# Splitting the projected queries and keys into two parts on GpSimd in SBUF instead of on ScalarE and VectorE out of PSUM

## The chip, the cores and the metric

The kernel runs on one core of one Trainium2 chip. The metric is the device time of one execution, in microseconds. The engines are named as the profile names them: PE (TensorE, matmuls), PEld (its weight loads), DVE (VectorE), ACT (ScalarE), POOL (GpSimd) and SP (SyncE, which here issues loads).

## What is computed

One layer of a decoder trunk on 2048 tokens of width 1024: sparse attention, then a SwiGLU feed-forward part, each followed by a layer norm of `alpha * x + sublayer(x)`. What matters here is the first half of the layer:

```
proj = h @ w_in                          # q (16 heads x 64) | c_kv (256) | q_idx (8 x 64) | k_idx (64) | w_idx (8)
c_kv = rms_norm(c_kv, g)
rel   = relu(einsum(q_idx * 64**-0.5, k_idx))     # per index head
score = sum over index heads of w_idx * rel       # causal
sel   = the 256 best keys of each query           # top-k
...
attention over the selected keys, logits from q, w_uk and c_kv, values from c_kv and w_uv
```

## The kernel before, in words

Matmuls that must be accurate in float32 are made of three: each operand is split into a high part `hi`, rounded to the type that PE multiplies (`F32R`), and a low part `lo`, the rest (value minus `hi`), and `mm3` (L208 to L214) adds up hi x hi, hi x lo and lo x hi in one PSUM bank, over the contraction in pieces of 128.

The tokens are done in four quarters of 512. For each quarter `index_part` (L273) transposes x, projects the index key and four tiles of index queries, and makes the compressed keys; `scores` (L323) makes the index scores of each block of 128 queries; `kv_part` (L359) makes eight tiles of keys and eight of values; `heads_part` (L349) projects the eight tiles of attention queries. Their order is given by the list ORDER: `i0 w0 k0 h0 i1 k1 i2 k2 i3 k3 h3 h2 h1` (i: index part and scores, w: weights of keys and values, k: keys and values, h: heads, with the number of the quarter).

A projected tile of 128x512 goes as follows. `load_split` (L158 on) brings 512 KB of weights by SP's queue and splits them on POOL: a scaled copy to `whi` (L166), then a subtraction to `wlo` (L137, in the helper `split_lo`). `mm3` makes 24 matmuls into one of two PSUM banks of the tag `mm`. Then `evac` (L258) takes the tile out: ACT copies it, scaled, to `evh` (L261), DVE computes the scaled value minus `evh` into `evl` (L262), reading PSUM again, and ACT's queue issues a store of each part to memory (L263, L264; `store` is `nc.scalar`). There are 80 such tiles: 16 of index queries (memory tensor `qis`), 32 of keys (`ks`), 32 of queries (`qs`). `evh` and `evl` have three buffers each (NEV = 3). The tag `evh` also serves the index key (L284) and the tag `evl` the value tiles (L377), which ACT copies to plain f32 (L378).

What stands beside it: the scores load the index queries back from `qis` by SP's queue (`qd`, L332), multiply (L338, two double banks `big`), ACT takes the result out through Relu (`rl`, L340), DVE adds it up into S (L343 for the first head, L345 for the others), and POOL masks the diagonal when a block is complete (L347). Top-k is a bisection on S: for some blocks of queries on DVE (count `jv` L412, step `g` L414 and `t` L415), for others on ACT (`ja` L423, `ga` L425, `ta` L426, started by a POOL memset, L405), with the preparation of the second search on POOL and DVE (L438, L440) and the selection at the end (L452 to L462). It is entered with a late priority. Attention (L465 on) follows from about 720 us; its copies of S to `sm` on POOL (L508) and the feed-forward part, where POOL makes `wl` (L137) and combinations of results that ACT's queue stores (L837), come later.

Waits, buffers and the order of the instructions on each engine come from a planner. It takes the program's order as priority (`later()` puts work behind everything else that is ready) and plays the program through with modelled times, giving each engine, as it comes free, the first instruction by priority that is ready; every engine, and every queue that issues DMAs, then works strictly in the order so found. All engines wait on the chip for the real end of what they depend on.

Of the kernel before, what the change touches and what calls it, by code (L numbers as in the profile page):

```python
# [11 lines left out]
F32 = mybir.dt.float32  # L12
F32R = mybir.dt.float32r
# [6 lines left out]
AF = mybir.ActivationFunctionType  # L20
ALU = mybir.AluOpType
# [4 lines left out]
P = 128  # L26
# [12 lines left out]
QUART = 512  # L39
# [9 lines left out]
NEV, NRL, NRAW = 3, 2, 2  # L49
# [23 lines left out]
def trunk(tc, x, w_in, w_uk, w_uv, kv_g, w_o, w_gu, w_down, lm_g, lm_b, lf_g, lf_b, out, stop=99):  # L73
    nc = tc.nc
# [55 lines left out]
    def f(ap):  # L130
        return ap.bitcast(F32)
# [4 lines left out]
    def split_lo(lo, src, hi, eng=None):  # L136
        (eng or nc.vector).tensor_tensor(out=lo, in0=src, in1=f(hi), op=ALU.subtract)  # L137
# [119 lines left out]

    def evac(pe, o, scale, dst, tok):  # L258

        hi, lo = (pe.tile([P, QUART], F32R, name=t, tag=t, bufs=NEV) for t in ("evh", "evl"))  # L260
        nc.scalar.activation(hi, o, AF.Copy, scale=scale)  # L261
        nc.vector.scalar_tensor_tensor(lo, o, scale, f(hi), op0=ALU.mult, op1=ALU.subtract)  # L262
        store.dma_start(out=dst[0, :, tok], in_=f(hi))  # L263
        store.dma_start(out=dst[1, :, tok], in_=f(lo))  # L264

# [7 lines left out]
    def index_part(pp, pq, pe, bk, st, t):  # L273
# [14 lines left out]
        for j in range(IH // 2):  # L288
            c0 = OFF_QI + j * P
            o = proj_tile(pp, bk, xx, [(lambda v: v, w3[:, :, c0:c0 + P])])  # L290
            evac(pe, o, 0.125, qis[:, j * P:(j + 1) * P], tok)
# [57 lines left out]
    def heads_part(pp, pe, bk, t, xx):  # L349

        t0 = t * QUART
        tok = slice(t0, t0 + QUART)
        if xx is None:
            xx = reloaded(pp, "x", xs[t], XB)
        for j in range(NPAIR):
            o = proj_tile(pp, bk, xx, [(lambda v: v, w3[:, :, j * P:(j + 1) * P])])
            evac(pe, o, 0.125, qs[j], tok)
# [643 lines left out]
    def pool(name, side="left"):  # L1001
        cm = tc.tile_pool(name=name, bufs=1, side=side, reuse_waits="tile")
        opened[name] = cm
        return cm.__enter__()
# [25 lines left out]
    with Banks("psb", big=(2, 2)) as big:  # L1030
        pe = pool("pe")
# [85 lines left out]
```

## Time and profile before

| | us |
|---|---|
| median of 3 runs (lowest, highest) | 3292.48 (3291.38, 3297.17) |
| the profiled execution, its own time | 3283.43 |
| its span, first to last instruction | 3281.7 |
| busy: PE | 3035.7 (93%) |
| busy: PEld | 2280.4 (69%) |
| busy: DVE | 2160.8 (66%) |
| busy: ACT | 1799.9 (55%) |
| busy: POOL | 1563.3 (48%) |

Busy time is an average over stages with different limits, so it has to be cut by stretches of the span. "Idle before" is the time for which an engine stood still ahead of an instruction, with the instruction that ended it. In a chain of waits, each piece is the work that the next one waited for. Spans of POOL are rough.

### The profile page before, as it was taken

The numbers are of one execution on the slowest core, as the hardware profiler recorded it, in microseconds if no ns is written. First come the engines' busy times: TensorE is split into PE (matmuls) and PEld (weight loads), VectorE is DVE, ScalarE is ACT, GpSimd is POOL, SyncE is SP. The second block draws the span as 40 slices with busy tenths as digits, with TensorE's granted clock in tenths as the row PEclk, the third lists the DMA queues.
The fourth block names the chain that finished last, engine by engine and source line by source line (L and its number), as shares of the span: only waits on it lengthen the run. The fifth ranks groups of instructions, "written<-read, shape, count | busy, mean of one in ns | idle before, by whom it ended". The sixth has DMA issues, their size and how long they took to land.

```text
span 3281.7 us, 45310 instructions
## 1 busy us (share of the span) xinstructions
PE 3035.7 (93%) x15067; PEld 2280.4 (69%) x15067; DVE 2160.8 (66%) x3304; ACT 1799.9 (55%) x3536; POOL 1563.3 (48%) x1309
## 2 busy tenths in 40 slices
PE   8988888878888889999999989999989999999996
PEld 6766776655555556666557767888868888888875
DVE  4749979998899545544436676555676555346289
ACT  2646886797899997766662223333333333333333
POOL 3424224543232334433325546666776666645475
PEclk9999999989899999999999999999989999999998
DMA  9776554644344543766536744322233222655353
GB/s 302 226 229 202 183 183 150 219 138 107 99 131 128 136 133 112 201 159 169 153 109 206 232 133 141 107 99 100 99 121 116 103 100 100 211 165 172 111 162 135
DMA packets 460442, 499.00 MB, mean 152 GB/s; under 512 B 51120, under 2 KB 331824, under 8 KB 460208
## 3 DMA queue, kind: packets, MB, share of 16 engines
q1 hardware_dynamic: 368992, 359.09, 38.0%
q10 hardware_dynamic: 91216, 137.01, 11.5%
q8 instruction: 120, 1.97, 0.3%
q14 instruction: 114, 0.93, 0.1%
HBM read 359.01 MB, written 136.97 MB: 151 GB/s over the span
## 4 chain that ended last, share of the span: by engine, by line
PE 62%; DVE 18%; ACT 6%; DMA 6%; issue 4%; POOL 1%; SPq 1%; ACTq 0%; DVEq 0%; POOLq 0%
PE mm L213 9%; PE mm L212 9%; PE mm L214 9%; PE oc L545 7%; PE tp L541 7%; PE big L518 6%; DVE jv L412 3%; PE mm L910 2%; PE mm L908 2%; PE mm L909 2%; ACT ja L423 2%; DVE S L345 2%; ACT sm L523 1%; PE mm L691 1%; DMA aqd<-qs 1%
## 5 line engine op out<-in xcount | busy, mean ns | idle before, releaser
L508 POOL TENSOR_SCALAR sm<-S 128x768 f32<-128x768 f32 (+7 forms) x384 | 334.9, 879 | 625.8 <-PE tp L541 556.2
L212 PE MATMUL mm<-ch,wh 128*128 128x512 f32 x1232 | 484.9, 395 | 15.0 <-ACT ch L721 14.5
L213 PE MATMUL mm<-cl,wh 128*128 128x512 f32 x1232 | 489.8, 398 | 8.8 <-DVE cl L137 7.4
L214 PE MATMUL mm<-ch,wl 128*128 128x512 f32 x1232 | 486.3, 395 | 0.0
L519 DVE CUSTOM_DVE_ANT_0 sm<-big,sm 128x1024 f32<-128x1024 f32 (+7 forms) x256 | 233.8, 921 | 226.5 <-POOL sm L508 136.7
L543 ACT COPY pt<-tp 128x512 f32<-128x512 f32 (+1 forms) x559 | 303.7, 567 | 143.9 <-PE tp L541 131.0
L523 ACT ACTIVATE sm<-sm,mx 128x768 f32<-128x768 f32 (+7 forms) x384 | 346.1, 910 | 44.9 <-DVE mx L519 44.6
L541 PEld LDWEIGHTS tp<-ident,sm 128*128 128x128 f32 x2176 | 237.0, 143 | 188.0 <-issue 178.2
L541 PE MATMUL tp<-ident,sm 128*128 128x128 f32 x2176 | 362.6, 290 | 2.7 <-ACT pt L543 1.8
L423 ACT ACTIVATE ja<-S,ta 128x896 int8<-128x896 int16 (+7 forms) x224 | 317.3, 1416 | 30.6 <-DVE evl L262 8.6
L137 POOL TENSOR_TENSOR wl<-s,wh 128x512 fp32r<-128x512 f32 x176 | 239.1, 1364 | 193.5 <-ACT wh L774 193.5
L412 DVE TENSOR_SCALAR_CACHE_REDUCE jv<-S,t 128x640 int8<-128x640 int16 (+7 forms) x224 | 302.9, 1352 | 4.3
L518 PE MATMUL big<-kka,aqd 128*128 128x512 f32 (+3 forms) x896 | 237.5, 388 | 58.9 <-DMA aqd<-qs 27.9
L774 ACT CAST wh<-s 128x512 fp32r<-128x512 f32 x176 | 109.0, 620 | 331.6 <-PE mm L214 94.3
L212 PEld LDWEIGHTS mm<-ch,wh 128*128 128x128 f32 x1232 | 233.5, 190 | 72.6 <-ACT ch L721 18.3
L213 PEld LDWEIGHTS mm<-cl,wh 128*128 128x128 f32 x1232 | 234.2, 190 | 64.6 <-DVE cl L137 11.7
L214 PEld LDWEIGHTS mm<-ch,wl 128*128 128x128 f32 x1232 | 234.2, 190 | 49.3 <-POOL wl L137 0.2
L545 PE MATMUL oc<-pt,vva 128*64 128x256 f32 (+1 forms) x1536 | 236.2, 402 | 25.1 <-ACT pt L543 19.6
L137 POOL TENSOR_TENSOR wl<-wr,wh 128x512 fp32r<-128x512 f32 x132 | 190.5, 1444 | 93.9 <-ACT wh L774 92.5
L137 POOL TENSOR_TENSOR cl<-hx,ch 128x512 fp32r<-128x512 f32 (+2 forms) x106 | 153.2, 1448 | 152.3 <-ACT ch L903 132.8
L518 PEld LDWEIGHTS big<-kka,aqd 128*128 128x128 f32 x896 | 156.9, 199 | 95.4 <-DVE mx L519 48.4
L903 ACT CAST ch<-hx 128x512 fp32r<-128x512 f32 (+2 forms) x158 | 95.0, 611 | 215.7 <-PE tp L909 95.2
(279 smaller groups left out, 6794.9 us busy)
## 6 DMA issues: line engine op xcount, KB each, us to landing
wr<-in_f_w_gu SPq DMA_DIRECT2D x44, 1024.0 KB, 5.1
gs<-cc ACTq DMA_DIRECT2D x154, 256.0 KB, 2.0
hx<-gs SPq DMA_DIRECT2D x144, 256.0 KB, 3.0
aqd<-qs SPq DMA_DIRECT2D x256, 128.0 KB, 3.2
wraw<-in_a_w_in SPq DMA_DIRECT2D x56, 512.0 KB, 4.3
kka<-ks SPq DMA_DIRECT2D x96, 256.0 KB, 4.3
hx<-in_f_w_down SPq DMA_DIRECT2D x66, 256.0 KB, 3.0
qd<-qis SPq DMA_DIRECT2D x112, 128.0 KB, 4.4
```

What stands on the lines that cost most here:

```text
L137: (eng or nc.vector).tensor_tensor(out=lo, in0=src, in1=f(hi), op=ALU.subtract)
L212: nc.tensor.matmul(o, lhsT=lh, rhs=rh, start=(i == 0), stop=False)
L213: nc.tensor.matmul(o, lhsT=lh, rhs=rl, start=False, stop=False)
L214: nc.tensor.matmul(o, lhsT=ll, rhs=rh, start=False, stop=(i == n - 1))
L412: nc.vector.tensor_scalar(out=junk[:, :L], in0=data(b), scalar1=t[b], scalar2=lim - (L - TOPK), op0=ALU.is_lt, op1=ALU.add, accum_out=col( ...
L423: nc.scalar.activation(junk[:, :L], data(b), AF.Sign, bias=t[b], scale=-1.0, accum_out=ca)
L508: nc.gpsimd.tensor_scalar(out=sm[:, :wn], in0=S[b0 + i][:, w0:w0 + wn], scalar1=slope, scalar2=1.0, op0=ALU.mult, op1=ALU.mult)
L518: nc.tensor.matmul(o[:, s0:s0 + n], lhsT=qd[:, c, i * P:(i + 1) * P], rhs=kk[wi_][e][:, s0:s0 + n], start=(c == 0), stop=(c == 1))
L523: nc.scalar.activation(sm[:, :wn], sm[:, :wn], AF.Exp, bias=mx[:, i, nw - 1:nw], scale=-1.0, accum_out=su[:, i, e, wi_:wi_ + 1])
L541: nc.tensor.transpose(tp[:, at:at + P], prob(e, i, kb), ident)
L543: pcopy(pt[:, :2 * n], tp[:, :2 * n])
L545: nc.tensor.matmul(ob[e * HD:(e + 1) * HD, i0 * P:256], lhsT=vv[kb][:, e * HD:(e + 1) * HD], rhs=pt[:, e * n:(e + 1) * n], start=(kb == 0) ...
```

## The change

`evac` alone is changed. ACT copies the PSUM tile, scaled, to a plain f32 tile `raw`, which has the buffers of the tag `evl`. POOL then copies it to `hi` (tag `evh`), rounded, and subtracts: `lo` = `raw` - `hi`, written over `raw` in place. `lo` is the same memory read as F32R. DVE no longer takes part, and PSUM is read once. The two stores, their order and their queue stay.

```diff
     def evac(pe, o, scale, dst, tok):
 
-        hi, lo = (pe.tile([P, QUART], F32R, name=t, tag=t, bufs=NEV) for t in ("evh", "evl"))
-        nc.scalar.activation(hi, o, AF.Copy, scale=scale)
-        nc.vector.scalar_tensor_tensor(lo, o, scale, f(hi), op0=ALU.mult, op1=ALU.subtract)
+        raw = pe.tile([P, QUART], F32, name="evl", tag="evl", bufs=NEV)
+        hi = pe.tile([P, QUART], F32R, name="evh", tag="evh", bufs=NEV)
+        lo = raw.bitcast(F32R)
+        nc.scalar.activation(raw, o, AF.Copy, scale=scale)
+        nc.gpsimd.tensor_scalar(out=hi, in0=raw, scalar1=1.0, scalar2=1.0, op0=ALU.mult, op1=ALU.mult)
+        split_lo(lo, raw, hi, nc.gpsimd)
         store.dma_start(out=dst[0, :, tok], in_=f(hi))
         store.dma_start(out=dst[1, :, tok], in_=f(lo))
```

`split_lo(lo, src, hi, eng)` (L136, L137) is one subtraction, `eng.tensor_tensor(out=lo, in0=src, in1=f(hi), op=ALU.subtract)`; `f` reads a tile as plain f32.

## Rows read from the trace of the kernel before

**Rows 1.** The page's second part: the span in 40 equal slices of 82 us, one digit each, the busy tenths of TensorE's matmuls and of VectorE.

```profile
PE   8988888878888889999999989999989999999996
DVE  4749979998899545544436676555676555346289
```

**Rows 2.** Busy time of each engine by stretch of the span (start:end in us, its length, then busy us and the number of instructions of each engine, granted TensorE clock, DMA share and GB/s).

```profile
0.00:280.00 280.00, 236.01 (x1078) 187.22 (x1079) 165.87 (x324) 133.31 (x303) 93.56 (x105) 0.95 0.83 255
280.00:720.00 440.00, 385.07 (x1724) 309.49 (x1722) 411.44 (x578) 353.30 (x734) 174.14 (x124) 0.95 0.55 171
1240.00:3282.00 2042.00, 1978.72 (x9628) 1510.11 (x9624) 1170.71 (x1669) 842.93 (x1514) 1111.91 (x871) 0.98 0.45 141
```

**Rows 3.** The chain of waits, its shares by line, first of 0 to 280 us and then of 280 to 720 us.

```profile
by line: DMA qd<-qis 10.7%; PE mm L212 9.6%; PE mm L213 9.3%; PE mm L214 9.0%; DMA wraw<-in_a_w_in 6.6%; issue 6.4%; DMA S<-in_x 4.4%; PE big L338 4.2%; ACT ja L423 3.6%; SPq L332 2.9%; DMA wlo<-wkv 2.7%; DMA xs<-xl 2.6%; POOL wlo L137 2.6%
...
by line: DVE jv L412 18.3%; DVE S L345 14.6%; issue 10.1%; DVE g L414 5.0%; DVE evl L262 4.7%; PE mm L212 4.2%; DVE t L415 3.9%; PE mm L213 3.8%; PE mm L214 3.7%; PE big L338 3.6%; DVE S L343 2.5%; DVE S L440 2.5%; DVE ft L459 2.2%; ACT rl 
```

**Rows 4.** The instructions of line 262 over the whole span (times are min/median/max in ns), and who waited for them (us, number of waits).

```profile
L262 DVE SCALAR_TENSOR_TENSOR evl<-mm,evh x80: 666/687/693, 28.7 to 710.7; 128x512 fp32r<-128x512 f32 x80
...
  PE mm L212: 17.9, 19
  ACT ga L425: 10.2, 6
  ACT ja L423: 8.6, 3
...
  ACT ta L426: 3.8, 3
  ACT rl L340: 1.7, 2
```

**Rows 5.** Groups of instructions by line, 0 to 720 us: the copy of the value projections, out of PSUM to plain f32 (busy us, mean ns of one, idle before).

```profile
L378 ACT COPY ve<-mm 128x512 f32<-128x512 f32 x32 | 18.8, 587 | 9.1 <-PE mm L214 2.7 <-issue 2.4 <-DVE S L433 2.3
```

**Rows 6.** VectorE's busy time on line 262 alone, 280 to 720 us (the columns of rows 2).

```profile
280.00:720.00 440.00, 32.87 (x48) 0.95 0.55 171
```

**Rows 7.** Groups of instructions on GpSimd with 128x512 tiles: the one scaled copy of that shape from 0 to 720 us, and the page's subtractions in the feed-forward part.

```profile
L508 POOL TENSOR_SCALAR sm<-S 128x512 f32<-128x512 f32 x1 | 0.6, 617 | 0.1
...
L137 POOL TENSOR_TENSOR wl<-s,wh 128x512 fp32r<-128x512 f32 x176 | 239.1, 1364 | 193.5 <-ACT wh L774 193.5
```

**Rows 8.** The timeline (start us, duration us, engine, line), first with GpSimd busy, then with GpSimd idle.

```profile
605.27 3.24 POOL L137 TENSOR_TENSOR wlo<-wraw,whi 128x1024 fp32r<-128x1024 f32 x1
606.80 1.74 DVE L414 TENSOR_SCALAR g<-cnt 128x2 f32<-128x2 f32 x1
...
690.84 0.16 DVE L414 TENSOR_SCALAR g<-cnt 128x2 f32<-128x2 f32 x1
691.04 0.16 DVE L415 SCALAR_TENSOR_TENSOR t<-g,t 128x2 f32<-128x2 f32 x1
691.11 1.28 DVE L345 SCALAR_TENSOR_TENSOR S<-rl,wi,S 128x1024 f32<-128x1024 f32 x1
```

**Rows 9.** Groups by line and shape on VectorE, 280 to 720 us.

```profile
L345 DVE SCALAR_TENSOR_TENSOR S<-rl,wi,S 128x1024 f32<-128x1024 f32 x24 | 33.8, 1411 | 0.0
L414 DVE TENSOR_SCALAR g<-cnt 128x2 f32<-128x2 f32 x55 | 31.4, 570 | 0.6
L415 DVE SCALAR_TENSOR_TENSOR t<-g,t 128x2 f32<-128x2 f32 x55 | 20.5, 373 | 1.3
```

**Rows 10.** Groups by line and shape on GpSimd, 280 to 720 us: the split of the weights.

```profile
L137 POOL TENSOR_TENSOR wlo<-wraw,whi 128x1024 fp32r<-128x1024 f32 x33 | 88.5, 2683 | 2.4
L166 POOL TENSOR_SCALAR whi<-wraw 128x1024 fp32r<-128x1024 f32 x33 | 41.2, 1248 | 118.6 <-PE mm L213 85.7 <-PE mm L214 32.8
L137 POOL TENSOR_TENSOR wlo<-wraw,whi 128x1056 fp32r<-128x1056 f32 x4 | 10.5, 2615 | 0.3
```

**Rows 11.** The instructions of line 837 over the whole span, GpSimd results that ScalarE's queue stores, and who waited for them (us, number of waits).

```profile
L837 POOL TENSOR_TENSOR cc<-cc x88: 1282/1297/1747, 1997.7 to 2831.4; 128x512 f32<-128x512 f32 x88
...
  ACT wh L774: 31.3, 21
```

**Rows 12.** The timeline of GpSimd where projection tiles follow each other closely (idle time before an instruction and what ended it in brackets).

```profile
46.90 1.08 POOL L166 TENSOR_SCALAR whi<-wraw 128x1056 fp32r<-128x1056 f32 x1 [2.24 <-PE mm L214]
48.06 2.47 POOL L137 TENSOR_TENSOR wlo<-wraw,whi 128x1056 fp32r<-128x1056 f32 x1
52.16 1.08 POOL L166 TENSOR_SCALAR whi<-wraw 128x1056 fp32r<-128x1056 f32 x1 [1.63 <-PE mm L213]
```

**Rows 13.** From the instructions that touch the tile evl: its stores' time from issue to landing.

```profile
DMA to landing us min/median/max: 2.3/4.2/7.4
```

**Rows 14.** The instructions of line 261 in the four bursts of key projections (min/median/max ns, first and last start).

```profile
L261 ACT ACTIVATE evh<-mm x8: 598/599/602, 76.7 to 91.4; 128x512 fp32r<-128x512 f32 x8
...
L261 ACT ACTIVATE evh<-mm x8: 593/598/639, 224.1 to 249.8; 128x512 fp32r<-128x512 f32 x8
...
L261 ACT ACTIVATE evh<-mm x8: 623/712/787, 349.7 to 368.1; 128x512 fp32r<-128x512 f32 x8
...
L261 ACT ACTIVATE evh<-mm x8: 581/601/636, 463.9 to 482.0; 128x512 fp32r<-128x512 f32 x8
```

**Rows 15.** Who waited for whom from 0 to 720 us (us in total, times, longest us).

```profile
POOL S L347 <- DVE S L345: 84.9, 7, 21.3
...
PE mm L212 <- POOL whi L166: 4.3, 2, 3.5
```

## The prediction

> **What bounds the kernel now.** I read the slices of the page first: up to about 1240 us PE stands at 7 to 9 tenths, mostly 8, with VectorE (DVE) at 9 for long runs; after that PE is at 9 or more nearly throughout [rows 1]. So the part before 1240 us is the one that can give time back. I cut it where the work changes [rows 2]. Up to 280 us (projections of the first half of the tokens) PE is busy 236.0 us and DVE 165.9. From 280 to 720 us (the other projections and the index scores, with top-k as filler) DVE is busy 411.4 of 440 us, 94%, GpSimd (POOL) only 174.1. After 720 us the changed lines no longer run; after 1240 us PE is busy 1978.7 of 2042 us. The chain of waits says the same [rows 3]: in the first stretch it runs through loads and matmuls, and its largest item is the reload of index queries (qd), 10.7%; in the second its largest items are DVE's, jv L412, S L345, g L414, and the instruction that the change removes, evl L262, has 4.7%.
>
> How evl hurts [rows 4]: there are 80, of 687 ns. PE waited for them 17.9 us in 19 waits, because they are the last readers of a PSUM bank and there are two banks; ScalarE (ACT) waited 10.2 + 8.6 + 3.8 + 1.7 = 24.3 us, because the store of the low part stands in ACT's queue ahead of other work.
>
> **The change, part by part.** A difference of under 0.2%, 6.6 us, counts as no change: about what a measurement of this kernel can tell.
>
> ACT's copy keeps its 128x512 form, about 600 ns now [rows 14]; a copy to plain f32 of that form took 587 ns [rows 5]. Nothing.
>
> Removed from DVE: 80 x 0.687 = 55 us, of which 48 instructions, 32.9 us, in the stretch that DVE bounds [rows 6].
>
> Added to POOL: a scaled copy of 128x512, 0.62 us, and a subtraction of 128x512, 1.36 us [rows 7]: 1.98 us a tile, 158 us in all, 95 us of it between 280 and 720 us, where POOL then has 174 + 95 = 269 of 440 us. There is room. What the work costs others is in the next items.
>
> DVE pays for a busy POOL. The two-element instruction g L414, started at 606.80 us while POOL's wlo (605.27, 3.24 us) ran, took 1.74 us and ended 0.03 us after it; with POOL idle, at 690.84 us, it took 0.16 [rows 8]. Over the second stretch that makes, for g, 55 x (570 - 160 ns) = 22.6 us, for t L415, 55 x (373 - 160) = 11.7, for the widest S, 24 x (1411 - 1280) = 3.1: 37 us lost [rows 8, 9], beside 140 us of whi and wlo on POOL [rows 10]. By busy time the new work would cost 37 x 95 / 140 = 25 us. But a DVE instruction waits only for what is left of POOL's, so the loss goes with the square of POOL's length: 48 x (0.62² + 1.36²) = 107 against 37 x (1.25² + 2.68²) = 323, a third, 12 us. I take 22, near the upper end, because the narrower S are left out of the 37. The removed evl itself was never stretched, 666 to 693 ns [rows 4]. So DVE's net is -33 + 22 = -11 us (-21 to -8). Projections and scores wait for S; jv is filler. S has 14.6% of the chain beside jv's 18.3% [rows 3], a share of 0.44, so -5 us counts (-9 to -3.5).
>
> [...] If POOL's 95 us blocked DVE for all their length, DVE's -11 would be +62 us; the rows above show 37 us for 140, not 140.
>
> PE's bank comes free at the end of ACT's copy instead of evl's. Late next is the copy itself, behind ACT's other work. Of 17.9 us I let 3 stay: -15 us (-18, or only -5 if ACT itself gets late).
>
> ACT's queue: both stores wait for POOL now, the second for 1.98 us at least, and behind them stand rl L340, for which the scores wait, the top-k steps and the next copy. The nearest row is POOL's L837, whose result ACT stores: 88 instructions for which ACT waited 31.3 us [rows 11], 0.36 each. 80 x 0.36 = 28 us in place of 24: +4. Bounds: no such wait, -24; 0.36 for each of the two steps, 57 us, +33. I take one wait a tile because the wait of the first store is part of the second's.
>
> POOL behind PE: where tiles follow each other closely, POOL spends 3.55 us a tile on weights and waits 2.24 and 1.63 us for PE in between [rows 12]. The new 1.98 us just fill that gap: +2 us over the few such tiles (0, or +8 where DVE slows POOL).
>
> Index queries go to memory and back before the scores: their low part leaves 0.62 + 1.36 - 0.69 = 1.3 us later, once for each of four quarters, and the reload is on the chain [rows 3]: +4 us (0 if other PE work covers it, +12 with POOL inside a wlo). No DMA is added, and the queue that issues them is the same; SP's queue holds nothing of the change but that reload.
>
> The raw tile takes a place in the ring of three that held evl, from ACT's copy to the landing: 0.6 + 0.62 + 1.36 + 4.2 us to land [rows 13] = 6.8, or 2.3 us a tile. In the four bursts of eight key tiles the copies start 2.1, 3.7, 2.6 and 2.6 us apart on average [rows 14], so only the first is held up: 7 x 0.2 = 1.4, say +2 us (with every landing at 7.4 us, 3.3 a tile: 7 x (1.2 + 0.7 + 0.7) = +18).
>
> Sum: -15 - 5 + 4 + 2 + 4 + 2 = -8 us. The profiled execution took 3283.43 us, for a span of 3281.7; it lies 9 us below the median of the three runs, 3292.48, and I apply the difference to the median: 3284.5 us.
>
> **Rivals.** *ACT stands behind POOL* (slower). The place is the second store: POOL works in order, and when it sits in a wlo, or in L347, which waited for DVE up to 21.3 us [rows 15], the pair comes late and all of ACT with it. Price: ACT +33, bank only -12, DVE -5, the three small items +8: +24, 3316.5 us. It decides from the point where the pair ends, on average, later after the copy than evl does now. For it: POOL stood 84.9 us in L347. Against it: PE lost only 4.3 us to whi from the same queue [rows 15].
>
> *The lock eats it* (no change). It costs 25 us, DVE nets -8, of which -3.5 counts; the bank gives -10, because ACT's copies stand behind rl, and rl behind S; the other items +12: -1.5, 3291 us. For it: 37 us are lost already. Against it: the new instructions are half as long. [...]
>
> *The bank does not come free sooner* (slower; the change then does less than it says). The ring of three is full, and the copy waits for a landing. Landings of 7.4 us cost +18 for +2: -8 + 16 = +8, 3300.5 us. For it: the first burst is already at 2.1 us. Against it: the median landing.
>
> *All of it is collected* (faster). Bank -18, DVE -9, half of ACT's 24, -12, small items +4: -35, 3257.5 us. For it: DVE at 94%. Against it: it needs every favourable bound at once.
>
> **How the numbers follow.** Forecast, a small gain: 0.42, of which 0.11 ends under 6.6 us, since it lies only 1.4 us beyond; all collected 0.10; lock 0.20; ACT behind POOL 0.22; ring 0.06. Faster 0.31 + 0.10 = 0.41; same 0.11 + 0.20 = 0.31; slower 0.28. The forecast's own range is 3272 to 3290 us. The range for 8 in 10 takes in the larger gain almost whole and the ACT rival: 3258 to 3318 us; it is also that wide because the order on every engine is planned anew from modelled times.
>
> **What would show it.** Between 280 and 720 us: no evl on DVE and DVE's busy time some 11 us lower, g and t longer on average than 570 and 373 ns; PE's waits for evl gone, with no like sum for the copy; ACT's waits for the two POOL steps near 28 us; a slightly larger share of qd in the first chain. I am wrong if ACT waits for POOL 50 us or more, if copies wait for landings of stores, if PE waits for whi or wlo more than some 10 us, or if the stretches after 720 us change their length.

## The result and the profile after

The changed kernel takes 3335.26 us (median of 4, 3333.15 to 3342.36) where the kernel before takes 3291.93 (median of 4): 1.0132 times as long, 95% interval 1.0110 to 1.0155, some 43 us slower. The forecast was 3284.5 us, a small gain; 3335 also lies above the range. The profiled executions stand at 3334.10 us (span 3332.3) and 3283.43 us, 50 us apart. In the changed kernel every line number behind `evac` is 3 higher than before (S L348, rl L343, g L417, t L418); the copy is L263, the two GpSimd steps L264 and L137 (tile evl).

The page's slices of the changed kernel, 83 us each, here with GpSimd's row, and below them busy time by stretch (columns as in [rows 2]).

```profile
PE   7887888887788899999999999999989999999996
DVE  3649979997989636444445666555585555336289
POOL 4754457674333334433333636666676666645475
```

```profile
0.00:280.00 280.00, 229.34 (x1036) 181.73 (x1037) 141.09 (x276) 126.64 (x292) 156.20 (x167) 0.93 0.81 250
280.00:720.00 440.00, 381.63 (x1689) 300.51 (x1689) 411.67 (x516) 332.70 (x692) 281.14 (x204) 0.96 0.54 167
720.00:1240.00 520.00, 420.60 (x2467) 266.40 (x2465) 407.01 (x726) 464.69 (x975) 177.16 (x212) 0.90 0.43 120
1240.00:3340.00 2100.00, 2025.02 (x9880) 1540.30 (x9878) 1195.27 (x1708) 877.48 (x1580) 1138.42 (x887) 0.98 0.45 140
```

Against [rows 2], PE has 42 matmuls fewer done by 280 us and some 76 by 720 us. VectorE, which lost 48 subtractions in the second stretch, is as busy in it as before (411.67 us for 411.44) with 62 instructions fewer: its time was not freed, it was refilled. ScalarE does 20.6 us less work there, so top-k falls behind (its last count on ScalarE ends at 1243 us instead of 1206), and the attention stage that follows is late too. Over the whole span PE is busy 3056.6 us instead of 3035.7 for the same matmuls: the granted clock fell from 0.968 to 0.959 of full speed in the mean. That is 21 of the 50 us; PE's idle time, 275.7 us instead of 246.0, is the other part.

The waits to 760 us, by engine, picked out (us in total, times, longest).

```profile
PE big L341 <- ACT rl L343: 40.1, 40, 3.9
...
PE mm L212 <- POOL whi L166: 12.1, 5, 5.8
PE mm L212 <- ACT evl L263: 11.3, 9, 2.3
...
PE mm L214 <- POOL wlo L137: 8.8, 7, 2.2
...
ACT rl L343 <- DVE S L348: 41.5, 27, 5.5
...
ACT evl L263 <- POOL evl L137: 7.7, 4, 3.5
...
DVE S L346 <- POOL wi L310: 19.5, 1, 19.5
```

Two chains are to be seen. VectorE's S is late, so ScalarE waits 41.5 us for it (24.1 before) to refill the two buffers of rl, and the scores' matmuls wait 40.1 us for rl (26.5 before). And GpSimd's other products are late: PE waits 12.1 and 8.8 us for the two parts of weights (4.3 and 2.1 before, the first in [rows 15]), and S waits 19.5 us for wi, a small scaling on GpSimd of the index heads' weights (6.5 before). That one wait costs PE little by itself: PE was busy 17.7 of the 19.5 us, with projections. Nor do such rows prove a loss: e1 below has a good part of them (ScalarE 36.9 us for S, PE 15.8 for weights, S 13.8 for wi) and is faster than the kernel before.

GpSimd's own steps, to 760 us, and what they waited for; the last line is the landing time of the tile's stores.

```profile
L264 POOL TENSOR_SCALAR evh<-evl x80: 608/625/2068, 29.2 to 745.2; 128x512 fp32r<-128x512 f32 x80
L137 POOL TENSOR_TENSOR evl<-evl,evh x80: 1261/1298/2816, 29.9 to 747.0; 128x512 fp32r<-128x512 f32 x80
...
  ACT evl L263: 76.4, 25
...
DMA to landing us min/median/max: 2.3/3.4/7.8
```

The shortest and the median steps are those of [rows 7], but the longest are 2 to 3 times as long: in the mean a copy took 0.88 us and a subtraction 1.51. And the queue of GpSimd, which works in order (a subtraction whose copy ended at 331.58 us ran only at 336.66, behind a step of top-k that had stood 3.47 us for VectorE), stands 76.4 us in front of the copies that it waits for.

VectorE to 720 us: S, the subtraction, g and t, picked out (busy us, mean ns, idle before), first before the change, then after it.

```profile
L345 DVE SCALAR_TENSOR_TENSOR S<-rl,wi,S 128x768 f32<-128x768 f32 (+5 forms) x161 | 169.7, 1064 | 21.4 <-ACT rl L340 20.4
...
L262 DVE SCALAR_TENSOR_TENSOR evl<-mm,evh 128x512 fp32r<-128x512 f32 x80 | 54.9, 687 | 48.1 <-ACT evh L261 41.4 <-DMA qd<-qis 4.8 <-DMA ks<-evl 1.6
L414 DVE TENSOR_SCALAR g<-cnt 128x2 f32<-128x2 f32 (+1 forms) x92 | 37.0, 402 | 1.5
L415 DVE SCALAR_TENSOR_TENSOR t<-g,t 128x2 f32<-128x2 f32 (+1 forms) x92 | 36.3, 395 | 2.3
```

```profile
L348 DVE SCALAR_TENSOR_TENSOR S<-rl,wi,S 128x768 f32<-128x768 f32 (+5 forms) x153 | 184.0, 1210 | 32.8 <-ACT rl L343 31.6
...
L418 DVE SCALAR_TENSOR_TENSOR t<-g,t 128x2 f32<-128x2 f32 (+1 forms) x88 | 50.6, 575 | 2.2
L417 DVE TENSOR_SCALAR g<-cnt 128x2 f32<-128x2 f32 (+1 forms) x88 | 35.2, 400 | 1.7
```

At the counts of before, the longer S and t cost 161 x 0.146 + 92 x 0.180 = 40 us: of the 54.9 us that left VectorE, 15 are truly gone. The timeline (start us, length us) shows one such case.

```profile
582.80 2.01 POOL L137 TENSOR_TENSOR evl<-evl,evh 128x512 fp32r<-128x512 f32 x1
...
583.58 1.25 DVE L418 SCALAR_TENSOR_TENSOR t<-g,t 128x2 f32<-128x2 f32 x1
```

t, two columns wide, ends 0.02 us after GpSimd's subtraction; and that subtraction, 2.01 instead of 1.26 us long, had itself been held up: the S before it had run from 582.15 to 583.66. Both sides pay.

### The profile page after: what moved, and what is told of

Its sections match the earlier page's. It is cut to its first block, busy times and chain, and to the rows that moved or that the text cites. A ratio compares the mean times of both kernels' runs of the same rounds, so it can differ in the third digit from the quotient of the medians.

```text
span 3332.3 us, 45438 instructions
## 1 busy us (share of the span) xinstructions
PE 3056.6 (92%) x15067; PEld 2288.9 (69%) x15067; DVE 2155.0 (65%) x3224; ACT 1801.5 (54%) x3536; POOL 1752.9 (53%) x1469
## 3 DMA queue, kind: packets, MB, share of 16 engines
q10 hardware_dynamic: 91216, 137.01, 11.3%
## 4 chain that ended last, share of the span: by engine, by line
PE 64%; DVE 17%; DMA 6%; issue 5%; ACT 5%; POOL 3%; SPq 0%; ACTq 0%; DVEq 0%; POOLq 0%
PE mm L212 9%; PE mm L214 9%; PE mm L213 9%; PE oc L548 8%; PE tp L544 7%; PE big L521 6%; DVE jv L415 3%; PE mm L913 3%; PE mm L911 3%; PE mm L912 3%; DVE S L348 2%; DMA aqd<-qs 2%; ACT ja L426 1%; DVE cl L137 1%; PE mm L694 1%
## 5 line engine op out<-in xcount | busy, mean ns | idle before, releaser
L212 PE MATMUL mm<-ch,wh 128*128 128x512 f32 x1232 | 492.2, 401 | 16.3 <-ACT ch L724 14.9
L137 POOL TENSOR_TENSOR wl<-s,wh 128x512 fp32r<-128x512 f32 x176 | 238.6, 1360 | 193.2 <-ACT wh L777 193.2
L137 POOL TENSOR_TENSOR wl<-wr,wh 128x512 fp32r<-128x512 f32 x132 | 190.5, 1444 | 97.8 <-ACT wh L777 92.7
L137 POOL TENSOR_TENSOR cl<-hx,ch 128x512 fp32r<-128x512 f32 (+2 forms) x106 | 154.7, 1463 | 149.5 <-ACT ch L906 128.2
L348 DVE SCALAR_TENSOR_TENSOR S<-rl,wi,S 128x768 f32<-128x768 f32 (+5 forms) x161 | 196.8, 1230 | 32.8 <-ACT rl L343 31.6
```

Of the source, the lines that this page charges most:

```text
L212: nc.tensor.matmul(o, lhsT=lh, rhs=rh, start=(i == 0), stop=False)
```

## The experiments

Five ideas stood against each other: ScalarE stands behind GpSimd at its stores; the two engines hold each other up (stretching, the lock of the expectations); GpSimd's queue brings its other products late; it is the removal that is worth little; each tile has a fixed price. "Taken out" kernels, which do not compute the low part, tell the worth of the removal apart from the price of the added work. All results, with GpSimd's busy time and the mean S (147 to 161 of them) from 0 to 720 us of each profile:

| kernel | median us | ratio to before (95%) | GpSimd us | S ns |
|---|---|---|---|---|
| before | 3291.9 | 1 | 267.7 | 1064 |
| changed | 3335.3 | 1.0132 (1.0110 to 1.0155) | 437.3 | 1210 |
| e1_no_lo | 3283.9 | 0.9975 (0.9956 to 0.9994) | 277.0 | 1162 |
| e2_no_lo_pair | 3325.3 | 1.0094 (1.0060 to 1.0129) | 442.2 | 1225 |
| e3_no_lo_pair_prev | 3328.9 | 1.0111 (1.0080 to 1.0142) | 440.5 | 1246 |
| e4_stores_sp | 3338.9 | 1.0139 (1.0108 to 1.0169) | 442.3 | 1237 |
| e5_no_lo_memsets | 3311.8 | 1.0052 (1.0034 to 1.0070) | 428.0 | 1170 |
| e6_pool_late_heads | 3313.6 | 1.0056 (1.0032 to 1.0080) | 326.2 | 1124 |
| e7_pool_all_else | 3313.9 | 1.0059 (1.0036 to 1.0082) | 385.6 | 1192 |
| e8_lo_on_dve | 3321.4 | 1.0088 (1.0061 to 1.0115) | 315.8 | 1113 |
| e9_no_lo_tiny | 3293.4 | 0.9995 (0.9978 to 1.0011) | 299.2 | 1171 |
| e10_reload | 3275.6 | 0.9956 (0.9939 to 0.9973) | 180.2 | 1039 |
| e11_reload_pool | 3259.0 | 0.9907 (0.9894 to 0.9919) | 233.4 | 1058 |
| e12_quarters | 3357.7 | 1.0202 (1.0183 to 1.0221) | 489.7 | 1175 |
| e13_reload_all | 3292.1 | 0.9996 (0.9984 to 1.0008) | 356.2 | 1168 |
| e14_reload_no_lo | 3242.9 | 0.9848 (0.9834 to 0.9861) | 180.7 | 1055 |
| e15_reload_later | 3276.8 | 0.9956 (0.9941 to 0.9971) | 321.7 | 1141 |
| e16_reload_first | 3279.3 | 0.9959 (0.9944 to 0.9974) | 223.5 | 1052 |
| e17_reload_dve_time | 3271.4 | 0.9942 (0.9922 to 0.9962) | 184.8 | 1048 |
| e18_reload_dve_lumps | 3272.4 | 0.9949 (0.9930 to 0.9967) | 189.7 | 1033 |

Differences between two experiments are differences of their ratios, times 3292 us; each ratio is to the runs of the kernel before on the same chip; such a difference carries some 6 to 15 us of uncertainty, and every kernel has its own planned order.

**e1_no_lo**: only the removal.

```diff
-        hi, lo = (pe.tile([P, QUART], F32R, name=t, tag=t, bufs=NEV) for t in ("evh", "evl"))
+        hi = pe.tile([P, QUART], F32R, name="evh", tag="evh", bufs=NEV)
         nc.scalar.activation(hi, o, AF.Copy, scale=scale)
-        nc.vector.scalar_tensor_tensor(lo, o, scale, f(hi), op0=ALU.mult, op1=ALU.subtract)
         store.dma_start(out=dst[0, :, tok], in_=f(hi))
-        store.dma_start(out=dst[1, :, tok], in_=f(lo))
+        store.dma_start(out=dst[1, :, tok], in_=f(hi))
```

> The kernel before with VectorE's step taken out and nothing put in its place: the low part is not computed, and the high part is stored twice. It prices the removal alone. My theory: the removal itself is worth something, 10 to 35 us (VectorE 55 us less, PE's 17.9 us of waits for evl gone), so 3257 to 3282 us, and the 43 us that the change lost come from what it adds on GpSimd. The rival, that the new order of the plan or the earlier release of the banks is itself harmful, wants 3300 us or more here.

The removal alone, with all that waited for the subtraction and no price paid, gives 0.0025, 8 us (2 to 14). It is not free of stretching: with no work added to GpSimd (busy 277.0 us for 267.7), the mean S grew from 1064 to 1162 ns and ScalarE's wait for S from 24.1 to 36.9 us. The added time of S lies beside the splits of weights, which are the same in both kernels: measured from the shortest instruction of each width, S lost 28 us beside whi and wlo in e1 and 13 us before. So these rows move without any added work; every kernel has its own order.

**e2_no_lo_pair** (behind e1's stores):

```diff
+        dm = pe.tile([P, QUART], F32, name="evl", tag="evl", bufs=NEV)
+        nc.gpsimd.tensor_scalar(out=dm, in0=f(hi), scalar1=1.0, scalar2=1.0, op0=ALU.mult, op1=ALU.mult)
+        split_lo(dm, f(hi), dm.bitcast(F32R), nc.gpsimd)
```

> The run without the low part, plus the pair of GpSimd instructions of the change, made from the high part into a tile that nobody reads; the stores do not wait for it. It holds everything that the change puts on GpSimd and nothing that waits for its results. If VectorE is shut out by GpSimd (lock) or GpSimd stands at the pair with the weights behind it (queue), this is as slow as the change, 3320 to 3340 us. If the stores, ACT's queue or the ring of three tiles that wait for the pair are the cause, it stays near the run without the pair, 3260 to 3290 us.

The pair's results are awaited by nobody (only its buffers are, for 2.3 us), and it still costs 0.0119, 39 us, of the 51 that separate the changed kernel from e1. What must be explained is mostly the price of GpSimd's time, not of waiting for its results. Nor are the weights late here: PE waits 10.8 us for whi and wlo, less than the 15.8 in e1, which is 39 us faster.

**e3_no_lo_pair_prev**: as e2, but the pair reads the tile before.

```diff
+        last = before.get("hi")
+        hi = before["hi"] = pe.tile([P, QUART], F32R, name="evh", tag="evh", bufs=NEV)
...
-        nc.gpsimd.tensor_scalar(out=dm, in0=f(hi), ...)
+        nc.gpsimd.tensor_scalar(out=dm, in0=f(last), ...)
```

> As the run with the unread pair, but the pair works on the high part of the tile before, which has long been in SBUF, so that GpSimd need not stand and wait for ACT's copy. Lock theory: VectorE is shut out as often, so as slow as the other pair run within 10 us. Queue theory: GpSimd's idle time at the pair (76.4 us for L264 in the changed kernel) and PE's waits for whi and wlo fall, and at least half of the difference between the pair run and the run without a pair goes.

This was meant to take away GpSimd's standing still for ScalarE's copy. It did not: the planner issues the pair as early as its order allows, and GpSimd's queue stood 98.9 us for evh. As a test of the queue it is inconclusive.

**e4_stores_sp**: the changed kernel, with both stores issued by SP's queue.

```diff
-        store.dma_start(out=dst[0, :, tok], in_=f(hi))
-        store.dma_start(out=dst[1, :, tok], in_=f(lo))
+        nc.sync.dma_start(out=dst[0, :, tok], in_=f(hi))
+        nc.sync.dma_start(out=dst[1, :, tok], in_=f(lo))
```

> The changed kernel with the two stores of a tile issued by SP's queue instead of ACT's, so that ACT never waits for GpSimd at a store. If ACT standing behind GpSimd is the cause (the rival of the prediction), most of the loss goes: 3295 to 3310 us. If it is the lock or the queue of GpSimd, it stays at 3325 to 3345 us, or gets slower where loads stand behind stores in SP's queue.

No gain. ScalarE's largest wait in this kernel, to 760 us, is again the one for S; but the waits for GpSimd's steps are not gone, they now stand in SP's queue, which issues the loads:

```profile
ACT rl L343 <- DVE S L348: 51.5, 36, 5.9
...
SPq L266 <- POOL evh L264: 118.0, 55, 7.7
SPq L267 <- POOL evl L137: 69.9, 49, 5.2
```

So this run alone does not clear the stores. e2 does for the greater part: there no store waits for GpSimd, and 39 of the 51 us stay. ScalarE behind GpSimd is not the main cause.

**e5_no_lo_memsets**: e3 with four writes in place of the pair, instructions of about 0.54 us that read nothing.

```diff
-        nc.gpsimd.tensor_scalar(out=dm, in0=f(last), ...)
-        split_lo(dm, f(last), dm.bitcast(F32R), nc.gpsimd)
+        for _ in range(4):
+            nc.gpsimd.memset(f(last), 0.0)
```

> As the run with the pair on the tile before, with four GpSimd memsets of 128x512 over that tile (after its stores) in place of the pair: GpSimd is held for about as long, but reads nothing from SBUF. The low part is not computed. Lock theory: S L345 and t L415 on VectorE, with two SBUF inputs, go free of the memsets, so most of the 45 us between the pair run (3328.9) and the run without a pair (3283.9) goes: below 3305 us, and S and t no longer on average than without a pair. Occupancy theory (GpSimd's time itself, weights and masks behind it): 3320 us or more.

The same GpSimd time costs 0.0077 over e1, 25 us, instead of e3's 45. VectorE to 720 us in e1, e2 and e5, a fence each:

```profile
L344 DVE SCALAR_TENSOR_TENSOR S<-rl,wi,S 128x768 f32<-128x768 f32 (+5 forms) x161 | 185.2, 1162 | 43.9 <-ACT rl L339 43.0
L413 DVE TENSOR_SCALAR g<-cnt 128x2 f32<-128x2 f32 (+1 forms) x96 | 38.4, 400 | 2.0
L414 DVE SCALAR_TENSOR_TENSOR t<-g,t 128x2 f32<-128x2 f32 (+1 forms) x96 | 30.8, 321 | 2.5
```

```profile
L347 DVE SCALAR_TENSOR_TENSOR S<-rl,wi,S 128x768 f32<-128x768 f32 (+5 forms) x153 | 185.5, 1225 | 34.8 <-ACT rl L342 34.1
L417 DVE SCALAR_TENSOR_TENSOR t<-g,t 128x2 f32<-128x2 f32 (+1 forms) x89 | 47.8, 537 | 2.5
L416 DVE TENSOR_SCALAR g<-cnt 128x2 f32<-128x2 f32 (+1 forms) x89 | 43.5, 489 | 1.7
```

```profile
L351 DVE SCALAR_TENSOR_TENSOR S<-rl,wi,S 128x768 f32<-128x768 f32 (+5 forms) x157 | 182.0, 1170 | 48.4 <-ACT rl L346 47.4
L420 DVE TENSOR_SCALAR g<-cnt 128x2 f32<-128x2 f32 (+1 forms) x92 | 50.1, 545 | 1.8
L421 DVE SCALAR_TENSOR_TENSOR t<-g,t 128x2 f32<-128x2 f32 (+1 forms) x92 | 35.0, 380 | 2.4
```

At e1's counts S, t and g are longer by 161 x 0.063 + 96 x (0.216 + 0.089) = 39 us beside the pair, and in the run with writes S is as long as in e1, t and g longer by 20 us. The means do not say what ran beside them; e5's timeline does (start us, length us; the shortest of these forms are 0.15 us for g and t, 1.13 for S).

```profile
656.75 1.70 POOL L270 MEMSET evh<- 128x512 f32 x3
...
657.20 0.15 DVE L421 SCALAR_TENSOR_TENSOR t<-g,t 128x2 f32<-128x2 f32 x1
657.27 1.15 DVE L351 SCALAR_TENSOR_TENSOR S<-rl,wi,S 128x896 f32<-128x896 f32 x1
...
689.64 2.01 POOL L270 MEMSET evh<- 128x512 f32 x4
...
690.12 0.60 DVE L420 TENSOR_SCALAR g<-cnt 128x2 f32<-128x2 f32 x1
...
690.75 0.16 DVE L421 SCALAR_TENSOR_TENSOR t<-g,t 128x2 f32<-128x2 f32 x1
```

All cases are like these. Beside writes alone, 35 S of 512 to 896 columns took at most 753, 1023 and 1153 ns, and 26 t at most 161 ns: as long as with GpSimd idle (752, 1020, 1153 and 163). g of two columns is held, 169 to 603 ns in 11 cases for 154 to 170 with GpSimd idle; g of one column is not (134 to 155). So writes themselves cost VectorE some 5 us, by g and the first head's S. What t and g lost beyond that stands for the most part beside whi and wlo: of 36 us for g of two columns 33. What else can make up the 25 us: all these instructions, each measured from the shortest of its form, lost 85 us beside the splits, 72 in e1; the memsets stood 93.6 us for landings of the tile's stores, for which the pair does not wait; and PE waited 24.6 us for whi and wlo. So part of the price is in what the pair reads, and not all of it.

**e6_pool_late_heads** and **e7_pool_all_else**: the kernel before with the change on the 24 tiles of attention queries of the last three quarters, and on the other 56 (`evac_dve` and `evac_pool` are the two forms of `evac`; in e7 the index queries and the keys use `evac_pool` too).

```diff
-            evac(pe, o, 0.125, qs[j], tok)
+            (evac_pool if t else evac_dve)(pe, o, 0.125, qs[j], tok)   # e6
+            (evac_dve if t else evac_pool)(pe, o, 0.125, qs[j], tok)   # e7
```

> The change made for the 24 tiles of attention queries of quarters 1 to 3 alone, which come after all keys, where VectorE is busiest and the tiles lie 8 to 9 us apart; the other 56 tiles as before. If the loss is proportional to the tiles, 24/80 of 43 us: 3305 us. If it comes from VectorE's shortage (lock where VectorE is the bound), more than its share: 3310 to 3325 us. If it comes from close tiles, where GpSimd has no gap left, none of it: 3285 to 3298 us.

> The change made for the other 56 tiles alone (index queries, keys, attention queries of quarter 0), the 24 late ones as before. By share of the tiles: 3325 us. Where VectorE's shortage decides: 3305 to 3318 us. Where the close tiles decide: 3330 us or more.

18 and 19 us: the two parts add up to 38 of the 43 us. The loss is not of one place. Per tile it is 0.77 us for the late ones and 0.35 for the others, a difference that is barely clear of the noise, and both results lie where VectorE's shortage wanted them.

**e8_lo_on_dve**: GpSimd makes `hi`, VectorE subtracts in SBUF.

```diff
-        split_lo(lo, raw, hi, nc.gpsimd)
+        split_lo(lo, raw, hi)
```

> The changed kernel with its second step back on VectorE: ACT copies the tile out whole, GpSimd makes the high part, VectorE subtracts in SBUF. GpSimd has 0.62 us a tile in place of 1.98, VectorE some 0.69 us again, now with two SBUF inputs, and the bank still comes free at the copy. If the price goes with GpSimd's time: some third of 43 us lost, plus the 8 us that the removal is worth: 3310 to 3320 us. If the subtraction's length is what shuts VectorE out: 3295 to 3308 us.

29 us slower, though GpSimd does only its scaled copy. VectorE's subtraction is the largest item, to 760 us:

```profile
L137 DVE TENSOR_TENSOR evl<-evl,evh 128x512 fp32r<-128x512 f32 x79 | 93.8, 1189 | 41.4 <-POOL evh L264 36.9 <-DMA wraw<-in_a_w_in 4.3
```

Reading PSUM it took at most 693 ns [rows 4]; with both inputs in SBUF, 1189 ns on average, 668 at the least and 692 in the median, so fewer than half are held, up to 2930 ns. What of the 29 us is the subtraction's and what belongs to the 48 us of GpSimd's copies is not separated.

**e9_no_lo_tiny** (behind e1's stores): GpSimd stands before each tile, but is held for one column.

```diff
+        dm = pe.tile([P, 1], F32, name="dmy", tag="dmy", bufs=NEV)
+        nc.gpsimd.tensor_scalar(out=dm, in0=f(hi)[:, 0:1], scalar1=1.0, scalar2=1.0, op0=ALU.mult, op1=ALU.mult)
```

> As the run without the low part, with one GpSimd instruction a tile that copies a single column of the high part to a tile nobody reads: GpSimd stands and waits for ACT's copy as in the changed kernel, but is held for some 0.2 us instead of 2. Standing theory (GpSimd in order, weights and masks behind the wait): 3305 us or more. Theory that GpSimd's time is what costs, by shutting VectorE out and by delaying its other work: within 8 us of the run without it, 3276 to 3292 us.

0.0020 over e1, 7 us and not clear of the noise, with GpSimd standing 79.4 us for evh from 280 to 720 us: standing is a small part at most.

**e10_reload** and **e11_reload_pool**: the first quarter's split weights of the attention queries are stored and reloaded by the other three quarters, 24 splits fewer on GpSimd; e11 adds e6's edit.

```diff
+            if t == 0:
+                wh, wl = load_split(...)
+                for i, v in enumerate((wh, wl)):
+                    store.dma_start(out=wq[j, i], in_=f(v).rearrange("p a b -> p (a b)"))
+            else:
+                ...
+                    nc.sync.dma_start(out=f(v)[:, :D], in_=wq[j, i])
```

> The kernel before, with the opposite done to GpSimd's time: the split weights of the attention queries are stored by quarter 0 and loaded by the quarters 1 to 3 (24 tiles, 3.75 us of GpSimd each, 90 us less; 24 x 0.5 MB more to load). If GpSimd's time costs what the pair's did (41 to 45 us for 158 us of it, more per tile in the late heads), taking 90 us away gains 15 to 35 us: 3260 to 3280 us. If only the change's own waits cost, or the added loads eat it: 3290 us or more.

> The run with reloaded weights, with the change made for the same 24 late tiles, so that GpSimd has 48 us more in a stretch where it has 90 us less. If the price is contention between GpSimd's instructions and VectorE (lock), the pair still costs, 5 to 12 us over the reload run; if it is GpSimd's other work coming late behind the pair, nothing is left to come late, and it is as fast as the reload run or up to 8 us faster, since VectorE has 16 us less.

The edit that cost 0.0056 in e6 now gains 0.0049, 16 us; the intervals of e10 and e11 lie apart. e11 leaves nothing of the computation out and beats both kernels: 0.9907 (0.9894 to 0.9919).

**e12_quarters**: each of the two steps in four pieces of 128 columns, so that a hold is shorter.

```diff
-        nc.gpsimd.tensor_scalar(out=hi, in0=raw, ...)
-        split_lo(lo, raw, hi, nc.gpsimd)
+        for c in range(4):
+            nc.gpsimd.tensor_scalar(out=hi[:, cs], in0=raw[:, cs], ...)
+        for c in range(4):
+            split_lo(lo[:, cs], raw[:, cs], hi[:, cs], nc.gpsimd)
```

> The changed kernel with each of the two GpSimd steps done as four instructions of 128 columns. GpSimd's time rises, by some 0.8 us a tile, but the longest hold falls from 1.3 us to 0.4. If VectorE loses by waiting for the rest of a GpSimd instruction, the loss goes with the square of its length and more than halves: 3305 to 3325 us. If GpSimd's total time counts: slower than the changed kernel, 3340 to 3360 us.

Slower still. t, g and S are a little shorter in sum (390, 508 and 1175 ns), but GpSimd is busy 52 us longer, and PE now waits 25.6 us for the copy and 14.4 for wlo. Beside the short steps alone VectorE's S (first heads included), t and g lost 15.9 us, beside the long ones of the changed kernel 33.9 (each from the shortest of its form). Short holds do hold VectorE up less; they do not save the kernel.

**e13_reload_all** and **e14_reload_no_lo**: the reload of e10 under the changed kernel, and under e1.

> The changed kernel, all 80 tiles by GpSimd, with the attention queries' weights split once and reloaded, which had taken 90 us of weight splits from GpSimd between 280 and 720 us and 19 us from the time of the kernel before (3275.6 us against 3294.5). Load of GpSimd: the price of a pair hangs on what else GpSimd has to do, so most of the 43 us goes: the change on top of the reload costs at most 10 us on the 3275.6 us (the late tiles gain 17, the others, which lie mostly where GpSimd keeps its weight splits, still lose): 3259 to 3286 us, with GpSimd busy under 240 us between 280 and 720 us and ScalarE's busy time to 720 us above 500 us. Price per tile: each pair costs about half a microsecond wherever it stands, so the change costs its 43 us again: 3319 us. The removal's side: PE loses bank time only in the close tiles of the first quarter: a rise within the first 280 us, none later.

> The kernel before with the reload and without VectorE's subtraction; both stores write the high part, so the low part of queries and keys is not computed. Load of GpSimd: the removal was worth only 8 us because the weight splits on GpSimd held VectorE up and late in other places; with 90 us of them gone the same removal is worth more, 15 to 25 us on 3275.6: 3251 to 3261 us, and the pair on all tiles then costs 10 to 30 us on top of it instead of 51. A fixed worth: 8 us again, 3268 us.

The removal is worth 0.0108, 36 us, on top of the reload, more than expected, and 8 without it. But the pair costs 0.0148, 49 us, as much as ever: "load sets the price of a pair" fell, and "load sets the worth of the removal" stood. VectorE's S and GpSimd's waits tell the same: S 1055 ns in e14, 1168 in e13, and S waits for wi 2.1 us in e14, 13.8 in e1.

**e15_reload_later** and **e16_reload_first**: on the reload, the change on the 60 tiles of the last three quarters, or on the first 20.

```diff
-  evac(pe, o, ...)                                # all three callers
+  (evac_pool if t else evac_dve)(pe, o, ...)      # e15; e16 the other way round
```

> The reload of the attention queries' weights, and the change on the 60 tiles of the last three quarters; the first quarter's 20 tiles keep VectorE's subtraction. With all 80 tiles changed on top of the reload the time was 3292.1, 16.5 us above the reload alone, and PE stood 19 us behind it by its 1500th matmul and 14 us behind by its 2700th. Place: the loss is made where the first quarter's tiles follow one another closely and GpSimd still splits weights for each; without those tiles it goes, and the later ones gain: 3255 to 3272 us. Price per tile: the loss is spread evenly, 60/80 of 16.5: 3288 us.

> The complement: the reload, and the change on the 20 tiles of the first quarter alone. Place: all of the loss and more, since the late tiles gained: 3288 to 3298 us, with PE more than 10 us behind the reload alone by its 1000th matmul (262 us against 250). Price per tile: 20/80 of 16.5: 3280 us.

Neither theory: both parts cost nothing in the end, while the whole costs 0.0040, 13 us. The place is right at first (busy time to 280 us of e10, then of e16):

```profile
0.00:280.00 280.00, 239.04 (x1089) 189.16 (x1090) 168.90 (x326) 136.30 (x307) 95.17 (x106) 0.95 0.90 286
```

```profile
0.00:280.00 280.00, 232.62 (x1040) 185.41 (x1040) 146.25 (x278) 125.66 (x290) 132.21 (x143) 0.91 0.87 274
```

49 matmuls are missing by 280 us and 45 still by 720 us, and the time is made good after that. Losses of this size in the first quarter are not final; parts of the change do not add up.

**e17_reload_dve_time** and **e18_reload_dve_lumps**: e14 with VectorE time put at S, evenly or in lumps, and no GpSimd work.

```diff
                     nc.vector.scalar_tensor_tensor(sv, rl[:, :wn], wi[:, h:h + 1], sv, ...)
+                dmv = pq.tile([P, 128], F32, name="dmv", tag="dmv", bufs=1)                                          # e17
+                nc.vector.scalar_tensor_tensor(dmv, rl[:, :128], 1.0, rl[:, 128:256], op0=ALU.mult, op1=ALU.add)     # e17
+                if h % 4 == 3:                                                                                       # e18
+                    nc.vector.scalar_tensor_tensor(rw, rw, 1.0, rw, op0=ALU.mult, op1=ALU.add)                       # e18, rw = rl[:, :wn]
```

> The kernel with the reload and without VectorE's subtraction (e14_reload_no_lo, 3242.9 us, ratio 0.9848; the low part of queries and keys is not computed), and after every S instruction of the scores a 128-column instruction on VectorE that reads the same rl and writes a tile that nobody reads. It is a price for VectorE's time in that place alone: GpSimd gets no work. 184 of them at some 0.3 us would be 55 us. Stretching theory: in the 16 runs so far, the time by which S, t and g were stretched comes back in the result at 1.2 us per us, and the subtraction itself only at 0.4; so time put at S costs about 1.2 times its length: about 3309 us for 55 us (1.2 times what the trace shows of it). Ordinary work: VectorE's time has one price, that of the subtraction, 0.4: 3265 us. GpSimd's time: the price hangs on GpSimd's busy time and not on VectorE's: 3243 us.

> As e17_reload_dve_time (the reload, no subtraction on VectorE, so the low part of queries and keys is not computed, and no added GpSimd work), but VectorE's added time stands in lumps: after the fourth and the eighth head of a block one instruction as long as S (about 1.06 us, 46 of them, 49 us in all) in place of 0.34 us after every head (62.9 us in all, which cost 28 us, or 0.45 per us). GpSimd's holds also come in lumps, of half to one and a half microseconds. Lumps: with only two buffers for rl, uneven S instructions stop the scores' matmuls where even ones do not; the cost per us is clearly higher than 0.45, towards the 1.2 of the stretched time: 3243 + 59 = 3302 us, at least 3280. Amount: only the sum of VectorE's time counts: 3243 + 49 x 0.45 = 3265 us, and then the rest of the price of GpSimd's work is not VectorE's.

e17's added work, to 720 us:

```profile
L347 DVE SCALAR_TENSOR_TENSOR dmv<-rl 128x128 f32<-128x128 f32 x184 | 62.9, 342 | 2.2 <-ACT rl L340 2.1
```

62.9 us cost 0.0094, 31 us: 0.49 per us. In e18, 44.2 us (the sum of six shapes) cost 0.0101, 33 us: 0.75. The intervals of the two overlap, and 3272 us lies between the 3265 and the 3280 that were to tell them apart, so whether lumps are dearer stays open. What stands: VectorE's time at S costs 0.5 to 0.75 us per us, and not the 1.2 per us that a line through the first 16 results had given for stretched time.

## Why the prediction was wrong, point by point

**The bank and the worth of the removal: failed.** The step "Of 17.9 us I let 3 stay: -15 us", with VectorE's -33 us of the second stretch valued at 0.44, came to some -30 us for a removal without any price (-15 - 33 x 0.44, before the 24.3 us of ScalarE's waits). Measured: 8 us (e1). PE's waits for evl went, but 11.3 us stay behind the copy in the changed kernel and 7.6 in e1, not 3; S lost 14 us more beside the splits of weights; and GpSimd's products came next: S's wait for wi went from 6.5 to 13.8 us in e1 and PE's for whi and wlo from 6.4 to 15.8. With the reload these fall to 2.1 and 5.8 us, S loses 10 us beside splits, and the same removal gives 36 us (e14). How much of the missing 22 us each of these took is not shown. I had looked for what is late next only at the bank, and not at the queue that I was about to fill.

**VectorE's stretching: right in kind, too small.** "A third, 12 us ... I take 22" by the square of the length, for the second stretch. Measured to 720 us: 40 us, against 158 us of added steps that grew to 191 (80 x (0.880 + 1.505)). Of the 40, 9 are already in e1, where no steps were added; that leaves some 31 for the steps. What was mis-sized is which S are caught: I had raised 12 to 22 for the narrower S, but those of 512, 768 and 896 columns together lost more than the widest (128x1024: 1411 ns in [rows 9], 1745 after; 128x896 to 780 us: 1282, then 1545); only those of 256 and 384 columns stayed. And GpSimd is held up in turn, so that its holds grow. The square law itself is not refuted: for e12's quarters it gives 4 x (0.30² + 0.46²) against 0.62² + 1.30², 0.58 of the loss, and beside the steps alone 15.9 us for 33.9 were measured. VectorE's net of 15 us came near the -11 of the sum by luck: it is over two stretches, and contains the 9 us of e1. The share of 0.44 was nearly right (0.5 to 0.75 by e17 and e18).

**"There is room" on GpSimd: failed, the costliest step.** 269 of 440 us was forecast, 281 measured; the number was right and the reading wrong. The sum gave GpSimd's added time no price but what it costs VectorE (22 us at 0.44, some 10) and +2 for "POOL behind PE"; e2 shows 39 us for that time with nobody waiting for its results. GpSimd works in order, and its other products did come later: wi (+13 us of waiting by S), whi and wlo (+14.5 by PE). But the weights do not explain the price: 9.4 of those 14.5 us are in e1 too, which gains, and in e2 they are 4.4. The idle time of GpSimd that I counted as free was time in which it waited, ready, for PE and VectorE [rows 10, 12, 15]; behind the pair it waits for ScalarE, 76.4 us. The bound that I set, 10 us for whi or wlo, is passed with 20.9.

**ScalarE's stores: about right.** +4 was forecast, with 28 us of waits. ScalarE's waits for the two steps come to some 20 us in the trace, and moving the stores to SP's queue gave nothing (e4), though that moved the waits with them. The rival built on it gave 3316.5 us, the nearest to the result, but e2 leaves only some 12 us for all that waits for the steps' results.

**The ring: about right.** +2 was forecast; copies waited 5.0 us once for a landing of qis, as before the change, and 2.7 us for ks, with a median landing of 3.4 us. **qd: no larger part of the first chain** (6.8% for 10.7%).

**That the stretches after 720 us keep their work: failed.** The changed lines run to 747 us. From 720 to 1240 us the granted clock was 0.90 for 0.93 of full speed and PE finished 176 matmuls fewer. ScalarE had 27.3 us less work done by 720 us, and top-k ends 38 us later.

**What would have shown it.** Of the signs that I had named, PE's waits for evl went and t grew (590 ns for 373); VectorE's busy time did not fall (411.7 us for 411.4) and g did not grow (564 ns for 570). Of the signs of being wrong, PE's 20.9 us for whi and wlo and the changed stretches after 720 us came; ScalarE's 50 us did not.

**What is shown and what is not.** Shown: GpSimd's added time costs 39 us when nobody waits for it (e2) and 49 with the reload (e13 over e14). By rows, stretching explains 39 us of VectorE's time in e2 and 161 x 0.113 + 96 x (0.124 + 0.035) = 33 in e13, at 0.5 to 0.75 that is some 16 to 30 us: between a third and three quarters of the price. What makes up the rest stays open. S's longer wait for wi in e2, 29.8 for 13.8 us, and e5's 25 us, with some 5 us of holding by the writes themselves, point to the queue; PE's shorter wait for whi and wlo in e2 points away from it, and no run took GpSimd's queue away and left its holds. How much of each difference is the planner's new order is open as well; that the parts in e15 and e16 do not add up to e13 suggests some 10 us.

Which instructions were held is shown as well. S and t, with two inputs in SBUF, were not held by writes alone (e5, 61 cases: 35 S took at most 1153 ns, 26 t at most 161) and were by the pair (46 S of the changed kernel lost 14.6 us beside its two steps without a split). evl, with its other input in PSUM, never took more than 693 ns before the change: 675 to 693 in the 26 cases beside whi or wlo, 666 to 693 in the 53 with GpSimd idle. In e8, with both inputs in SBUF, it took up to 2930 ns.

## What to carry to other kernels

Before moving work to an engine with idle time, look at what that engine's queue delivers and how late it is allowed to be, and at which instructions of others the new work will run beside: here its idle time was readiness. Value a removal by taking it out alone, and the new place by adding work there that nobody waits for; two runs gave 8 against 39 us and would have decided this change. Where the engine is first relieved, here by reloading split weights, the same edit on 24 tiles turned from 18 us lost to 16 us gained.

## What the runs showed of the hardware that was not expected

GpSimd's 128x512 subtraction, 1.30 us in the median of the changed kernel, took up to 2.82 us, and its scaled copy, 0.62, up to 2.07; in the case of the timeline S ran beside it: both engines are held up, not VectorE alone. A GpSimd instruction that only writes held g, which reads one small operand in SBUF: with two columns it took 0.17 to 0.60 us beside writes alone for 0.15 to 0.17 beside an idle GpSimd, with one column never more than 0.155 (e5). And VectorE's subtraction with both inputs in SBUF grew from 0.69 to 1.19 us on average beside GpSimd (e8, median 0.69), so reading PSUM a second time was the cheaper form for VectorE.
